# Routing order, unread products and the weight tiles of the first layer in a two-layer mixer and expert kernel

## The chip, the cores and the metric

The kernel runs on 1 core of one Trainium2 chip. The metric is device time in microseconds (us), the median of the runs of one kernel; lower is better. All tensors are float32.

## The reference, cut to what matters

Two layers work on 512 latent rows and 256 context rows of 1024 columns. Each layer first mixes tokens (four head groups, output projection, gated residual) and then runs expert-choice experts, which the change touches:

```python
def expert_choice_ffn(x, router_w, wg, wu, wd):
    bn, n, _ = x.shape
    cap = CAPACITY_FACTOR * n // N_EXPERTS
    aff = jax.nn.softmax(jnp.einsum('bnd,de->bne', x, router_w).astype(jnp.float32), axis=-1)
    gate, idx = lax.top_k(aff.transpose(0, 2, 1), cap)
    bidx = jnp.arange(bn)[:, None, None]
    xg = x[bidx, idx]
    hid = jax.nn.silu(jnp.einsum('becd,edf->becf', xg, wg)) * jnp.einsum('becd,edf->becf', xg, wu)
    o = jnp.einsum('becf,efd->becd', hid, wd) * gate[..., None].astype(x.dtype)
    return jnp.zeros_like(x).at[bidx, idx].add(o)
```

There are 16 experts, and each takes the 64 best of the 512 latent rows and, in the first layer, the 32 best of the 256 context rows. The input of the experts is the RMS-normalised row, scaled and shifted by the conditioning. Each expert has three 1024 x 1024 matrices (gate, up, down), 4 MB each; the two layers read 96 of them. The context stream ends after the first layer, so layer 1 (the second) has latent rows alone.

## The kernel before, in words

**Mixers.** Each layer's front computes the projections, the four head groups and the output projection. Its last part, the loop over units `(t, n)`, takes one 128-row tile and 256 columns at a time: `wout_unit` makes the output projection (L1327) and adds it to the residual `X`, and `front_unit`, two units behind, squares the row for the norm (ACT L1345), transposes two 128 x 128 pieces (PE L1348) and multiplies them with the router's weights (PE L1355).

**Routing.** `willing(r)` (r = 0 latent, r = 1 context) turns the sums into the inverse norm (`rsqrt`: ACT L397 and L398, DVE L400 to L403), adds up the logits, and makes the softmax (ACT L1372 is its exponential, DVE L1380 its last step). `route` transposes the affinities (PE L1398), finds the best rows with rounds of max, match-replace and max-index on DVE (L1406 to L1409), and merges two half lists over PE (L1412, L1413, L1417) into row numbers (DVE L1427 to L1437). In layer 0, `fetch` then gathers the chosen rows from DRAM with an indirect DMA (POOL L1452), and `turned` scales a gathered row by its inverse norm (ACT L1464), transposes it (PE L1469), and applies scale and shift: the first four pieces of 128 columns on DVE (L1479), the other four on ACT (L1477). In layer 1 the rows are picked by a matrix product instead (PE L1494, L1472).

The context rows are routed first and gathered while the latent ones are still at work: `xg1 = fetch(1, 0)` stands in the loop, `willing(0)` and `route(True)` behind it, and the context rows are turned into `XC[0]` behind the mark `R0`, the transposes of the latent affinities.

**Experts.** In layer 0 each weight tile is multiplied with 64 latent rows (`lat_mm`, L1587) and 32 context rows (`ctx_mm`, L1595). The first expert's context products come before its latent ones. The hidden state is transposed again before the down matrix (`tr_lat` L1662, `tr_ctx` L1670 to L1671). Every matrix comes in four tiles (`CUTS`), each 1 MB: two rows of 1024 floats on each of 128 partitions. Partition p of a tile holds the neighbouring rows 2p and 2p + 1, so one partition is one piece of 8 KB. To match, whatever is multiplied with a weight tile is cut by `tile_of(k)`: every second column of 256, a slice with step 2.

**Order.** A framework schedules the recorded instructions of each engine by priority and by estimated readiness; each engine then runs its own list strictly in order. `tc.issue_after(x)` puts what is recorded inside it behind instruction x. The weight stream is issued from SP in a fixed order as the arena frees memory; in layer 0 it is held back behind the first gather of latent rows (`st.guard`, a POOL memset at L1562).

Of the kernel before, what the change touches and what calls it, by code (L numbers as in the profile page):

```python
# [226 lines left out]
def hybrid_kernel(ctx: ExitStack, tc: tile.TileContext, T, out):  # L227
# [11 lines left out]
    PS = psp.tile([128, 8, 512], F32, name="banks")  # L239
# [120 lines left out]
    def exp_item(l, e, w, k0, nk, n=None):  # L360

        src = T["exp_w_" + w][l, e]
        if n is None:
            src = src[k0 * 128:(k0 + nk) * 128].rearrange("(p k) f -> p k f", k=2)
            return ("exp", l, e, w, k0), (nk, 1024), lambda ap: sp.dma_start(ap, src)
        src = src[:, n * 512:(n + 1) * 512].rearrange("(q p j) f -> p q j f", p=128, j=2)
        if nk > 1:
            return ("exp", l, e, w, k0, n), (nk, 512), lambda ap: [
                sp.dma_start(ap[:, k:k + 2], src[:, (k0 + k) // 2]) for k in range(0, nk, 2)]
        return ("exp", l, e, w, k0, n), (nk, 512), lambda ap: sp.dma_start(ap[:, 0], src[:, k0 // 2, k0 % 2])  # L370
# [45 lines left out]

    def tile_of(k):

        return slice(k // 2 * 256 + k % 2, k // 2 * 256 + 256, 2)

# [30 lines left out]
    def ada_group(l, b, hf):  # L451
# [14 lines left out]
        for j in range(J):  # L466
            pe.transpose(tb[:, j * 128:(j + 1) * 128], M.v[:, tile_of(j) if b else slice(j * 128, (j + 1) * 128)],
                         ident)
# [63 lines left out]
    def layer(l):  # L532
# [807 lines left out]
        def front_unit(t, n):  # L1340

            r = 0 if t < 4 else 1
            t_ = t - 4 * r
            xs = X.v[:, t, n * 256:(n + 1) * 256]
            act.activation(sqr().v, xs, AF.Square, accum_out=SS[r][:, t_, n:n + 1])  # L1345
            tb = bank("T")
            for kk in range(2):
                pe.transpose(tb[:, kk * 128:(kk + 1) * 128], xs[:, tile_of(kk)], ident)  # L1348
            xt = xq().v
            if t % 2:  # L1350
                dve.tensor_copy(xt, tb[:, 0:256])
            else:
                act.activation(xt, tb[:, 0:256], AF.Copy)
            for kk in range(2):
                pe.matmul(LG[r][:, t_, n], xt[:, kk * 128:(kk + 1) * 128], rwa.v[:, r, 2 * n + kk, :],  # L1355
                          start=kk == 0, stop=kk == 1)

        def willing(r):
# [31 lines left out]
        def route(lat):  # L1390
# [6 lines left out]
            for j in range(nj):  # L1397
                pe.transpose(R[0:64, j * 128:(j + 1) * 128], afl[r].v[:, j].rearrange("p a b -> p (a b)"), ident)  # L1398
            marks["R%d" % r] = nc.cur_bb.bb.instructions[-1]
            wk, tops, tt = rbuf[r]  # L1400
            vals, ix, ixf = tops.v[0:64, 0], tops.v[0:64, 1].bitcast(U32), tops.v[0:64, 2]
# [53 lines left out]

        def turned(r, xg, d=None, halves=(0, 1)):

            d = d or (xtr if r == 0 else xtc)()
            fetched = isinstance(xg, Buf)
            for k4 in halves:  # L1460
# [4 lines left out]
                for kk in range(4):  # L1465
                    k = k4 * 4 + kk
                    o = tb[:, kk * 128:(kk + 1) * 128]
                    if fetched:
                        pe.transpose(o, xg.v[:, tile_of(k)], ident)  # L1469
                    else:  # L1470
                        for t in range(4):
                            pe.matmul(o, X.v[:, t, tile_of(k)], xg[:, t], start=t == 0, stop=t == 3)  # L1472
                for kk in range(4):
                    k = k4 * 4 + kk
                    a, b = modA[l][:, 1, k, r:r + 1], modT[l][:, 3, k, r:r + 1]
                    if k4:
                        act.activation(d.v[:, k, :], tb[:, kk * 128:(kk + 1) * 128], AF.Identity, scale=a, bias=b)  # L1477
# [69 lines left out]
        st.limit = AHEAD[1][l] + MORE[l]  # L1547
        st.pump()
        willing(0)
        rt[0] = route(True)  # L1550
        mp = latest(mybir.EngineType.PE)
        kinds["T"][0] = [5, 6]
        if cx:
            xg0 = fetch(0, 0)
            gi = latest(mybir.EngineType.Pool)
            with tc.issue_after(marks["R0"]):
                XC[0] = turned(1, xg1).v
            XG[0] = turned(0, xg0).v
# [100 lines left out]
        def tr_lat(h1):  # L1659
            tb = bank("T")  # L1660
            for j in range(4):
                pe.transpose(tb[:, j * 128:(j + 1) * 128], h1[:, tile_of(j)], ident)  # L1662
            a = ht()
# [4 lines left out]
        def tr_ctx(h2):  # L1668
            tb = bank("T")
            for i in range(4):  # L1670
                pe.transpose(tb[:, i * 64:(i + 1) * 64], h2[:, tile_of(i)], ident[0:64, 0:64])  # L1671
            c = htc()
# [303 lines left out]
def _arrays(v):  # L1976
# [11 lines left out]
    pack = lambda *ts: np.concatenate([t.reshape(t.shape[0], -1) for t in ts], 1)  # L1988
    a["c0"] = pack(np.eye(128, dtype=np.float32), cc, np.stack([rows(v["norm1_g"]), twos(v["norm2_g"])], 2))
    dg = np.stack([v["diff_qn_g"], v["diff_kn_g"]], 1)  # L1990
# [3 lines left out]
    for l in range(DEPTH):  # L1994
        rw = np.zeros((128, 8, 16), np.float32)
        rw[:] = v["router_w"][l].reshape(4, 128, 2, NE).transpose(1, 0, 2, 3).reshape(128, 8, NE)
        sgb = v["sgu_b"][l].reshape(2, 2, 128).transpose(1, 0, 2)
# [24 lines left out]
```

## Time and profile before

| | |
|---|---|
| median of 3 runs | 1990.66 us (1985.25, 1990.66, 2001.73) |
| profiled execution, its own time | 1998.31 us |
| its span, first to last instruction | 1996.2 us |
| mean granted TensorE clock | 0.963 |
| PE / DVE / ACT / POOL busy | 1818.0 / 898.0 / 651.6 / 226.7 us |
| experts of layer 0, products of latent rows | 546.9 to 1107 us |
| experts of layer 1, products | 1533.6 to about 1984 us |

The profile's busy times are averages over stages with different limits: the two fronts (to about 546 us, and from 1107 to 1533 us) are chains over several engines, the experts of layer 0 keep TensorE busy throughout, and those of layer 1 run at the pace of the weight stream. TensorE's granted clock has two levels, 1.0 (2.4 GHz) and 0.5 (1.2 GHz).

### The profile page before, as it was taken

To read this page: it belongs to the slowest core of one execution; us is meant where nothing else is said; L and a number is where in the kernel's file an instruction comes from. 1 tells how busy PE (TensorE), PEld (TensorE's weight loads), DVE (VectorE), ACT (ScalarE), POOL (GpSimd) and SP (SyncE) were. 2 spreads that over 40 slices of the span, in tenths; PEclk is the share of its full clock that TensorE was granted. 3 is DMA by queue.
4 is the path that set the end of the run, shared out by engine and by line. 5 is a ranking of instruction groups with operands and counts; after the bars stand their busy time and mean duration, and the time that the engine had idled before them with its cause. 6 is when DMAs were issued, how large, how long until landed. Compare 5 with 4: busy or idle time off the path is not lost.

```text
span 1996.2 us, 31498 instructions
## 1 busy us (share of the span) xinstructions
PE 1818.0 (91%) x13005; PEld 1028.0 (52%) x13005; DVE 898.0 (45%) x1885; ACT 651.6 (33%) x1386; POOL 226.7 (11%) x191
## 2 busy tenths in 40 slices
PE   5999988989699999999999799898896999988888
PEld 3786787679433333333333388596694333322322
DVE  3758564533523433433434565864434243223222
ACT  2456544532222322322222345654520221111101
POOL 0432033101000000000000043232010000000000
PEclk9999999979799999999999899998887999999999
DMA  9116135542599999988988212525727999999997
GB/s 337 55 50 199 43 114 173 194 147 85 197 413 393 384 336 358 377 331 340 365 335 331 82 43 94 168 93 195 274 102 252 421 421 421 421 422 422 422 422 306
DMA packets 131967, 525.98 MB, mean 263 GB/s; under 512 B 12240, under 2 KB 42864, under 8 KB 83184
## 3 DMA queue, kind: packets, MB, share of 16 engines
q1 hardware_dynamic: 129088, 514.00, 67.0%
q0 software_dynamic: 2736, 9.97, 1.3%
q8 instruction: 102, 1.67, 0.3%
q14 instruction: 41, 0.34, 0.0%
HBM read 513.40 MB, written 10.52 MB: 262 GB/s over the span
## 4 chain that ended last, share of the span: by engine, by line
PE 31%; DMA 16%; DVE 4%; ACT 2%; issue 1%; SPq 1%; POOL 0%; ACTq 0%; DVEq 0%; POOLq 0%
PE banks L1587 13%; DMA ar<-in_exp_w_gate 5%; DMA ar<-in_exp_w_up 5%; DMA ar<-in_exp_w_down 4%; PE banks L1595 3%; PE banks L1327 3%; PE banks L628 1%; DMA ar<-in_w_in 1%; PE banks L697 1%; PE banks L639 1%; PE banks L1718 1%; PE banks L1036 1%; PE banks L458 1%; PE banks L1719 1%; SPq L1030 1%
## 5 line engine op out<-in xcount | busy, mean ns | idle before, releaser
L1587 PE MATMUL banks<-ar,ar 128*32 128x512 f32 (+1 forms) x4576 | 713.6, 597 | 31.6 <-DMA ar<-in_exp_w_down 14.1
L1587 PEld LDWEIGHTS banks<-ar,ar 128*32 128x32 f32 (+1 forms) x4576 | 195.1, 119 | 454.6 <-issue 379.8
L1595 PE MATMUL banks<-ar,ar 128*32 128x512 f32 x1536 | 203.7, 605 | 0.0
L628 PE MATMUL banks<-ar,ar 128*128 128x256 f32 x1344 | 175.8, 287 | 2.0 <-DVE ar L807 1.5
L628 PEld LDWEIGHTS banks<-ar,ar 128*128 128x128 f32 x1344 | 166.7, 193 | 7.1 <-issue 2.6
L1327 PE MATMUL banks<-ar,ar 128*128 128x256 f32 x960 | 140.4, 302 | 1.9 <-ACT ar L1223 1.3
L1327 PEld LDWEIGHTS banks<-ar,ar 128*128 128x128 f32 x960 | 128.4, 204 | 4.0 <-ACT ar L1223 2.4
L1721 DVE TENSOR_TENSOR ar<-ar,banks 128x512 f32<-128x512 f32 x136 | 87.5, 683 | 67.5 <-PE banks L1719 67.2
L1595 PEld LDWEIGHTS banks<-ar,ar 128*32 128x32 f32 x1536 | 51.0, 112 | 117.3 <-issue 108.8
L1452 POOL DMA_INDIRECT ar<-rows,icoli x19 | 18.0, 949 | 783.0 <-ACT ar L1477 457.1
L408 ACT ACTIVATE ar<-banks 128x512 f32<-128x512 f32 x32 | 19.1, 597 | 255.4 <-PE banks L1587 255.4
L1685 DVE SCALAR_TENSOR_TENSOR ar<-banks,gcol,ar 64x512 f32<-64x512 f32 x62 | 46.5, 749 | 124.3 <-PE banks L1587 123.6
L571 POOL TENSOR_TENSOR ar<-ar,ar 128x2048 fp32r<-128x2048 f32 x14 | 64.7, 4625 | 180.1 <-ACT ar L570 166.4
L1477 ACT ACTIVATE ar<-banks,modT,modA 128x128 f32<-128x128 f32 x80 | 30.1, 456 | 167.6 <-PE banks L1469 136.3
L458 PE MATMUL banks<-ar,S 128*32 128x256 f32 x768 | 62.7, 403 | 21.2 <-DMA ar<-in_ada_w 20.2
L697 PE MATMUL banks<-ar,ar 128*128 128x512 f32 (+1 forms) x288 | 72.0, 397 | 4.8 <-DVE ar L598 2.0
L906 ACT ACTIVATE ar<-banks,mx 128x768 f32<-128x768 f32 (+1 forms) x80 | 65.2, 819 | 31.4 <-DVE mx L903 29.0
L411 DVE SCALAR_TENSOR_TENSOR ar<-banks,ar 128x512 f32<-128x512 f32 x32 | 21.9, 683 | 117.1 <-ACT ar L410 117.1
L903 DVE TENSOR_REDUCE mx<-banks 128x1 f32<-128x768 f32 (+1 forms) x80 | 66.6, 845 | 15.0 <-PE banks L898 12.1
L1656 DVE TENSOR_TENSOR ar<-banks,ar 64x512 f32<-64x512 f32 x32 | 21.7, 679 | 97.3 <-ACT ar L1601 97.3
L639 PE MATMUL banks<-ar,ar 128*128 128x512 f32 (+1 forms) x288 | 62.6, 372 | 2.4 <-ACT ar L815 2.3
L697 PEld LDWEIGHTS banks<-ar,ar 128*128 128x128 f32 x288 | 51.8, 197 | 17.5 <-DVE ar L582 2.8
(341 smaller groups left out, 2505.5 us busy)
## 6 DMA issues: line engine op xcount, KB each, us to landing
ar<-in_exp_w_gate SPq DMA_DIRECT2D x128, 1024.0 KB
ar<-in_exp_w_up SPq DMA_DIRECT2D x128, 1024.0 KB
ar<-in_exp_w_down SPq DMA_DIRECT2D x124, 1024.0 KB
ar<-in_ada_w SPq DMA_DIRECT2D x96, 512.0 KB
ar<-in_w_in SPq DMA_DIRECT2D x18, 1024.0 KB
ar<-in_w_out SPq DMA_DIRECT2D x8, 1024.0 KB
ar<-in_exp_w_down SPq DMA_DIRECT2D x7, 512.0 KB
ar<-in_rpb SPq DMA_DIRECT2D x8, 384.0 KB
```

The costliest lines, as they stand in the source:

```text
L458: pe.matmul(B[32 * q:32 * q + 32, 0:n], S[:, k, :], w[:, q * n:(q + 1) * n], start=k == 0, stop=k == 7)
L571: pool.tensor_tensor(lo, raw, hi.v, OP.subtract)
L628: pe.matmul(B[:, tt * 256:(tt + 1) * 256], a.r[:, k, t * 128:(t + 1) * 128], b[:, k, :], start=n == 0, stop=n == 23)
L639: pe.matmul(B[:, 0:n1 - n0], b[:, k, c * 128:(c + 1) * 128], a.r[:, k, n0:n1], start=n == 0, stop=n == 23)
L697: pe.matmul(PS[:, t, s], x.r[:, k, t * 128:(t + 1) * 128], w, start=k == 0 and i == 0, stop=k == 7 and i == 2)
L903: dve.tensor_reduce(mx, s, AX, OP.max, negate=True)
L906: act.activation(e, s, AF.Exp, bias=mx, accum_out=sm)
L1327: pe.matmul(B, a[:, c, t * 128:(t + 1) * 128], b[:, k, :], start=i == 0, stop=i == 23)
L1587: pe.matmul(B[n * 64 + j:n * 64 + j + p, :], xt[:, k, j:j + p], w[:, k - k0, n * 512:(n + 1) * 512], start=k == 0, stop=k == 7)
L1595: pe.matmul(B[j:j + 32, :], xt[:, k, :], w[:, k - k0, n * 512:(n + 1) * 512], start=k < 2, stop=k > 5)
L1685: dve.scalar_tensor_tensor(o[p0:p0 + 64, n * 512:(n + 1) * 512], B[s, :], gc[s, e:e + 1], G2.v[s, 0, n * 512:(n + 1) * 512], OP.mult, OP.mult)
L1721: dve.tensor_tensor(xs, xs, B, OP.add)
```

## The change

1. **Order in the routing of layer 0.** The exponential of the latent softmax is marked (`E0`), and the turning of the context rows is placed behind that mark too, no longer behind `R0` alone. The scale and shift of `XC[0]` all go to ACT (`spare=True`).
2. **Unread products.** `warm(n)` multiplies a piece of X with the identity n times, into a bank that nobody reads: twice ahead of `willing(0)` in both layers, and behind the transposes of the latent affinities four times in layer 0 and eight times in layer 1.
3. **Weight tiles of layer 0.** A tile's two rows per partition are p and p + 128, so that each 128-row tile is a block of neighbouring rows, and one partition is two pieces of 4 KB. `tile_of(k, l)` gives in layer 0 plain slices of 128 neighbouring columns; the norm gains, the router's weights and the conditioning are laid out to match. Layer 1 keeps its layout.

```diff
     def exp_item(l, e, w, k0, nk, n=None):
 
         src = T["exp_w_" + w][l, e]
+        if l + 1 < DEPTH:
+            src = src[k0 * 128:(k0 + nk) * 128].rearrange("(k p) f -> p k f", p=128)
+            return ("exp", l, e, w, k0), (nk, 1024), lambda ap: sp.dma_start(ap, src)
         if n is None:
             src = src[k0 * 128:(k0 + nk) * 128].rearrange("(p k) f -> p k f", k=2)
...
-    def tile_of(k):
-
+    def tile_of(k, l):
+
+        if l + 1 < DEPTH:
+            return slice(k * 128, (k + 1) * 128)
         return slice(k // 2 * 256 + k % 2, k // 2 * 256 + 256, 2)
...
+        def warm(n):
+
+            with tc.issue_after(latest(mybir.EngineType.PE)):
+                for _ in range(n):
+                    pe.matmul(PS[:, 1, :], ident, X.v[:, 0, 0:512], start=True, stop=True)
 
         def willing(r):
...
             act.activation(lgb, lgb, AF.Exp)
+            marks["E%d" % r] = latest(mybir.EngineType.Activation)
...
             marks["R%d" % r] = nc.cur_bb.bb.instructions[-1]
+            if lat:
+                warm(4 if cx else 8)
...
-        def turned(r, xg, d=None, halves=(0, 1)):
+        def turned(r, xg, d=None, halves=(0, 1), spare=False):
...
-                        pe.transpose(o, xg.v[:, tile_of(k)], ident)
+                        pe.transpose(o, xg.v[:, tile_of(k, l)], ident)
...
-                    if k4:
+                    if k4 or spare:
                         act.activation(d.v[:, k, :], tb[:, kk * 128:(kk + 1) * 128], AF.Identity, scale=a, bias=b)
...
         st.pump()
+        warm(2)
         willing(0)
         rt[0] = route(True)
...
-            with tc.issue_after(marks["R0"]):
-                XC[0] = turned(1, xg1).v
+            with tc.issue_after(marks["R0"]), tc.issue_after(marks["E0"]):
+                XC[0] = turned(1, xg1, spare=True).v
             XG[0] = turned(0, xg0).v
```

The same `tile_of(k, l)` stands in `front_unit`, `tr_lat`, `tr_ctx` and the conditioning's transposes (L467).

The lists of the engines show what the scheduler made of it. ScalarE (ACT) at the routing of layer 0, before; `n20y` is the inverse norm of the latent rows, `lg_4942` their logits, `ar_4042` the gathered context rows, `ar_4921` is `XC[0]`, `ar_4043` the first gathered latent rows, L1601 copies half of a context product:

```order
L397 ACTIVATE n20y<-n20v 128x4
L1464 ACTIVATE ar_4042<-ar_4042 128x512 x2
L398 ACTIVATE n20y<-n20y 128x4
L1372 ACTIVATE lg_4942<-lg_4942 128x64
L1477 ACTIVATE ar_4921<-banks,modT_73,modA_75 128x128 x4
L1601 ACTIVATE ar_4912<-banks 64x512
L408 ACTIVATE ar_4909<-ar_4912 64x512
L409 ACTIVATE ar_4909<-ar_4909 64x512
L410 ACTIVATE ar_4909<-ar_4909 64x512
L412 ACTIVATE ar_4909<-ar_4909 64x512
L1464 ACTIVATE ar_4043<-ar_4043 128x512 x2
L1601 ACTIVATE ar_4913<-banks 64x512
```

and with the change (line numbers are those of the changed kernel, L1478 is L1464 of before):

```order
L400 ACTIVATE n20y<-n20v 128x4
L401 ACTIVATE n20y<-n20y 128x4
L1383 ACTIVATE lg_4944<-lg_4944 128x64
L1478 ACTIVATE ar_4042<-ar_4042 128x512 x2
L1491 ACTIVATE ar_4921<-banks,modT_73,modA_75 128x128 x8
L1616 ACTIVATE ar_4912<-banks 64x512
L411 ACTIVATE ar_4909<-ar_4912 64x512
L412 ACTIVATE ar_4909<-ar_4909 64x512
L413 ACTIVATE ar_4909<-ar_4909 64x512
L415 ACTIVATE ar_4909<-ar_4909 64x512
L1616 ACTIVATE ar_4913<-banks 64x512
L1478 ACTIVATE ar_4043<-ar_4043 128x512 x2
```

The scaling of the gathered context rows stands behind the softmax's exponential, all eight pieces of `XC[0]` are ACT's, and the copy of the second context product (L1601, now L1616) has come ahead of the scaling of the first latent rows.

VectorE (DVE) at the end of the latent list of best rows in layer 0, before; L1656 and L411 belong to the first expert's context rows, `cand` and `icol` to the merged list:

```order
L1406 MAX ar_4005<-ar_4004 64x8
L411 SCALAR_TENSOR_TENSOR ar_4909<-ar_4912,ar_4909 64x512
L1409 MAX_INDEX ar_4005<-ar_4005,ar_4004 64x8
L1410 CAST ar_4005<-ar_4005 64x64
L1650 TENSOR_TENSOR ar_4909<-ar_4909,ar_4912 64x512
L1414 COPY ar_4006<-banks 64x128
```

and with the change:

```order
L1423 MAX_INDEX ar_4005<-ar_4005,ar_4004 64x8
L1671 TENSOR_TENSOR ar_4912<-banks,ar_4912 64x512
L1424 CAST ar_4005<-ar_4005 64x64
L1428 COPY ar_4006<-banks 64x128
L1441 COPY cand_4998<-banks 128x64
L1443 TENSOR_TENSOR late_4996<-cand_4998 128x16
L1444 SCALAR_TENSOR_TENSOR dif_4997<-cand_4998 128x16
L1452 TENSOR_TENSOR gcol_4995<-cand_4998 128x16
L1445 TENSOR_TENSOR dif_4997<-dif_4997,late_4996 128x16
L414 SCALAR_TENSOR_TENSOR ar_4909<-ar_4912,ar_4909 64x512
L1448 TENSOR_TENSOR icol_4994<-dif_4997,cand_4998 64x8 x2
```

L1656 (now L1671) moved from among the rounds to behind the last one, L411 (now L414) from ahead of the last round to just ahead of the row numbers, and L1650 behind them.

TensorE (PE) in the same place with the change; L1367 are the unread products, L1610 (L1595 before) the first context products:

```order
L1360 MATMUL banks<-ar_3989,ar_3997 128x16 x2
L1367 MATMUL banks<-ar_3918,c_68 128x512 x2
L1410 MATMUL banks<-c_68,ar_4002 64x128 x2
L1367 MATMUL banks<-ar_3918,c_68 128x512 x4
L1483 MATMUL banks<-c_68,ar_4042 128x128 x8
L1610 MATMUL banks<-ar_4054,ar_4921 32x512 x4
```

Apart from the two L1367 rows this list is as before: the four products stand ahead of the context rows' transposes.

## Rows read from the trace of the kernel before

**Rows 1.** The page, part 1: busy time (share of the span) and instructions.

```profile
PE 1818.0 (91%) x13005; PEld 1028.0 (52%) x13005; DVE 898.0 (45%) x1885; ACT 651.6 (33%) x1386; POOL 226.7 (11%) x191
```

**Rows 2.** Windows, experts of both layers: length, engines, PEclk, DMA share, GB/s.

```profile
546.88:1107.20 560.32, 557.07 (x4789) 189.18 (x4788) 222.09 (x357) 149.64 (x268) 8.43 (x9) 1.00 0.92 356
1550.00:1900.00 350.00, 319.92 (x1412) 112.51 (x1412) 104.40 (x171) 59.63 (x107) 6.61 (x7) 1.00 1.01 422
```

**Rows 3.** Timeline, softmax of layer 0: start, duration, instruction [idle before <-releaser].

```profile
514.40 0.20 ACT L397 ACTIVATE n20y<-n20v 128x4 f32<-128x4 f32 x1 [0.44 <-DVE n20v L395]
518.86 1.33 ACT L1464 ACTIVATE ar<-ar 128x512 f32<-128x512 f32 x2 [4.26 <-DMA ar<-rows,icoli]
520.10 0.19 ACT L398 ACTIVATE n20y<-n20y 128x4 f32<-128x4 f32 x1
...
523.37 0.63 PE L1398 MATMUL banks<-c,ar 128*64 128x128 f32 x2 [7.78 <-DVE ar L1380]
```

**Rows 4.** Timeline, layer 0, from the list of best rows to the first latent rows.

```profile
524.90 0.73 DVE L1479 TENSOR_SCALAR ar<-banks,modA,modT 128x128 f32<-128x128 f32 x2
...
525.75 1.50 ACT L1477 ACTIVATE ar<-banks,modT,modA 128x128 f32<-128x128 f32 x4 [3.16 <-PE banks L1469]
...
529.91 0.59 ACT L1601 ACTIVATE ar<-banks 64x512 f32<-64x512 f32 x1 [2.66 <-PE banks L1595]
...
531.94 0.66 DVE L1656 TENSOR_TENSOR ar<-banks,ar 64x512 f32<-64x512 f32 x1
...
535.35 0.67 DVE L411 SCALAR_TENSOR_TENSOR ar<-ar,ar 64x512 f32<-64x512 f32 x1
...
538.63 6.00 PE L1595 MATMUL banks<-ar,ar 128*32 128x512 f32 x32
...
539.88 0.17 DVE L1437 CAST icoli<-icol 128x8 int32<-128x8 f32 x1
...
545.59 1.36 PE L1469 MATMUL banks<-c,ar 128*128 128x128 f32 x8 [0.95 <-ACT ar L1464]
```

**Rows 5.** Timeline, the same steps in layer 1.

```profile
1503.90 0.20 ACT L397 ACTIVATE n20y<-n20v 128x4 f32<-128x4 f32 x1 [0.44 <-DVE n20v L395]
...
1507.91 0.63 PE L1398 MATMUL banks<-c,ar 128*64 128x128 f32 x2 [2.82 <-DVE ar L1380]
1518.20 0.31 PE L1412 MATMUL banks<-c,ar 64*64 64x64 f32 x1 [9.65 <-DVE ar L1406]
...
1521.86 0.17 DVE L1437 CAST icoli<-icol 128x8 int32<-128x8 f32 x1
...
1524.38 9.32 PE L1472 MATMUL banks<-ar,ar 128*128 128x128 f32 x56 [0.79 <-DVE ar L1496]
```

**Rows 6.** Windows of the two routings: columns as in Rows 2.

```profile
516.00:518.00 2.00, 0.00 (x0) 0.00 (x0) 0.06 (x1) 0.00 (x0) 0.00 (x0) 0.53 0.98 338
1528.00:1530.00 2.00, 2.00 (x11) 2.00 (x11) 0.00 (x0) 0.00 (x0) 0.00 (x0) 0.53 0.00 0
```

**Rows 7.** Timeline of PE, layer 1: products of this form, identity and X.

```profile
1945.15 1.02 PE L1744 MATMUL banks<-ar,c 128*128 128x512 f32 x2
1946.01 1.02 PE L1741 MATMUL banks<-ar,c 128*128 128x512 f32 x2
```

**Rows 8.** One line, L467: durations in ns (min/median/max) of weight loads.

```profile
L467 PEld LDWEIGHTS banks<-c,ar x24: 137/196/219, 26.4 to 1426.0; 128*128 128x128 f32 x24
```

**Rows 9.** Timeline of PE: transposes of step 2 (L1469, L1662) and of neighbouring columns (L920).

```profile
162.39 0.82 PE L920 MATMUL banks<-c,ar 128*128 128x128 f32 x6
...
173.07 0.60 PE L920 MATMUL banks<-c,ar 128*128 128x128 f32 x4
...
565.90 0.75 PE L1662 MATMUL banks<-c,ar 128*128 128x128 f32 x4
...
662.78 1.23 PE L1469 MATMUL banks<-c,ar 128*128 128x128 f32 x8
```

**Rows 10.** Lines, 546.88 to 1107.2 us, PE: count, busy us, mean ns.

```profile
L1469 PE MATMUL banks<-c,ar 128*128 128x128 f32 x81 | 12.6, 296 | 0.0
L1662 PE MATMUL banks<-c,ar 128*128 128x128 f32 x64 | 11.9, 308 | 0.0
```

**Rows 11.** Windows with short DMA pieces: columns as in Rows 2.

```profile
25.00:50.00 25.00, 21.58 (x140) 13.48 (x140) 10.44 (x26) 5.54 (x16) 2.51 (x2) 0.93 0.90 327
1960.00:1970.00 10.00, 9.21 (x40) 2.97 (x39) 1.38 (x2) 0.00 (x0) 0.00 (x0) 1.00 1.01 410
```

**Rows 12.** Waits, 545 to 1110 us: in total, times, longest.

```profile
PEld banks L1587 <- DMA ar<-in_exp_w_down: 1.3, 4, 0.4
```

More of the change, by code (lines that the diff above doesn't have):

```diff
@@ L466, in ada_group @@
         for j in range(J):
-            pe.transpose(tb[:, j * 128:(j + 1) * 128], M.v[:, tile_of(j) if b else slice(j * 128, (j + 1) * 128)],
+            pe.transpose(tb[:, j * 128:(j + 1) * 128], M.v[:, tile_of(j, l) if b else slice(j * 128, (j + 1) * 128)],
                          ident)
@@ L1347, in front_unit @@
             for kk in range(2):
-                pe.transpose(tb[:, kk * 128:(kk + 1) * 128], xs[:, tile_of(kk)], ident)
+                pe.transpose(tb[:, kk * 128:(kk + 1) * 128], xs[:, tile_of(kk, l)], ident)
             xt = xq().v
@@ L1468, in turned @@
                     if fetched:
-                        pe.transpose(o, xg.v[:, tile_of(k)], ident)
+                        pe.transpose(o, xg.v[:, tile_of(k, l)], ident)
                     else:
                         for t in range(4):
-                            pe.matmul(o, X.v[:, t, tile_of(k)], xg[:, t], start=t == 0, stop=t == 3)
+                            pe.matmul(o, X.v[:, t, tile_of(k, l)], xg[:, t], start=t == 0, stop=t == 3)
                 for kk in range(4):
@@ L1661, in tr_lat @@
             for j in range(4):
-                pe.transpose(tb[:, j * 128:(j + 1) * 128], h1[:, tile_of(j)], ident)
+                pe.transpose(tb[:, j * 128:(j + 1) * 128], h1[:, tile_of(j, l)], ident)
             a = ht()
@@ L1670, in tr_ctx @@
             for i in range(4):
-                pe.transpose(tb[:, i * 64:(i + 1) * 64], h2[:, tile_of(i)], ident[0:64, 0:64])
+                pe.transpose(tb[:, i * 64:(i + 1) * 64], h2[:, tile_of(i, l)], ident[0:64, 0:64])
             c = htc()
@@ L1988, in _arrays @@
     pack = lambda *ts: np.concatenate([t.reshape(t.shape[0], -1) for t in ts], 1)
-    a["c0"] = pack(np.eye(128, dtype=np.float32), cc, np.stack([rows(v["norm1_g"]), twos(v["norm2_g"])], 2))
+    a["c0"] = pack(np.eye(128, dtype=np.float32), cc, np.stack(
+        [rows(v["norm1_g"]), np.concatenate([rows(v["norm2_g"][:-1]), twos(v["norm2_g"][-1:])], 1)], 2))
     dg = np.stack([v["diff_qn_g"], v["diff_kn_g"]], 1)
@@ L1995, in _arrays @@
         rw = np.zeros((128, 8, 16), np.float32)
-        rw[:] = v["router_w"][l].reshape(4, 128, 2, NE).transpose(1, 0, 2, 3).reshape(128, 8, NE)
+        by = (4, 128, 2, NE) if l + 1 == DEPTH else (4, 2, 128, NE)
+        rw[:] = np.moveaxis(v["router_w"][l].reshape(by), by.index(128), 0).reshape(128, 8, NE)
         sgb = v["sgu_b"][l].reshape(2, 2, 128).transpose(1, 0, 2)
```

## The prediction, made before the changed kernel ran

> **What bounds the kernel now.** I read the page first: TensorE is busy 91% of the span [rows 1], but an average over four stages says nothing about the routing. The windows separate them [rows 2]. In the experts of layer 0 PE is busy 557.07 of 560.32 us while the DMA moves 356 GB/s; in those of layer 1 the DMA's share is 1.01 at 422 GB/s. So time saved on PE counts in the first of these stages and not in the second. The two routings lie ahead of them, and there the timeline shows which wait ends last.
>
> In layer 0 the latent softmax is held up by work that isn't its own: ACT does L397 at 514.40, then stands in front of L1464, which waits 4.26 us for the gathered context rows, and comes to L398 at 520.10. The affinities reach PE (L1398) at 523.37, 8.97 us after L397 [rows 3]. Layer 1 has the same steps and no gathered rows: there it is 1507.91 - 1503.90 = 4.01 us [rows 5]. The rounds that find the best rows then share DVE with foreign work: four pieces of L1479, L1656 and L411 stand among them [rows 4].
>
> PE rests in both routings and its clock falls: 0.53 in the mean at 516 to 518, where it has no product, and still 0.53 at 1528 to 1530, where it is busy again [rows 6].
>
> **The change, part by part.**
>
> *Softmax ahead of the scaling.* From L397 to L1398 I take layer 1's 4.01 in place of 8.97: -4.96 us, L1398 at 518.4. From L1398 to the row numbers (L1437) layer 0 takes 539.88 - 523.37 = 16.51 us and layer 1, on an undisturbed DVE, 1521.86 - 1507.91 = 13.95. By the new order L1656 and L411 still lie on this chain, 0.66 + 0.67: 15.28, so -1.23. Together L1437 comes at 533.7, **6.2 us earlier** [rows 3 to 5].
>
> The new wait is L1656 itself. It stands in the queue of the last step, behind it the cast, the merge and all that follows, and it needs the first context product, which now starts behind four unread products. One call of this form is two instructions, 1946.01 - 1945.15 = 0.86 us [rows 7]. From L1398's end at 519.0 PE needs 3.4 us, then 1.2 for eight transposes [rows 9]; ACT, 0.6 us in, takes 8 x 0.375 = 3.0 (four took 1.50), and L1601 began 2.66 us behind the last of these [rows 4]. So L1656 is ready near 529.3. DVE reaches it 10.3 us after L1398 by layer 1's pace (1518.20 - 1507.91 [rows 5]) and a last index search later, 529.1. There is no margin, so I count -6.0.
>
> Behind L1437 the gather is as before: 545.59 - 539.88 = 5.7 us to the first transposes of latent rows. The second context batch, 6.00 us before [rows 4], and its copy, which now stands ahead of the scaling on ACT, must fit under it: PE starts them once the merge is off it, some 2 us ahead of L1437, so near 531.7; they end by 537.7 and the copy, 0.59, by 538.3; the scaling, 0.7 us ahead of the first transposes as for the context rows, would begin at 533.7 + 5.7 - 0.7 = 538.7. This cover is thin too. The POOL memset that lets the weight stream go on sits behind the same gather, so it moves with it, and SP's queue with that.
>
> *Pieces of XC[0] to ACT.* Four pieces leave DVE (0.73 for two, [rows 4]); that gain is in the 1.23 above. ACT has 1.5 us more, counted above.
>
> *Unread products.* PE's pauses ahead of L1398 begin at 523.37 - 7.78 = 515.6 and at 1505.1 [rows 3, 5]. Two calls, 1.7 us, lie in what remains of them, up to 518.4 and 1507.9. In layer 1 eight calls, 6.9 us from 1508.5, are done at 1515.4, ahead of L1412 at 1518.20 [rows 5, 7]. All of it is in pauses: cost 0. If PE ran them at the low level, eight would take 13.8 us, end at 1522.3 and hold L1412 up by 4.1 us. What they can give is bounded by L1472: 9.32 us for 56, of which the part to about 1530 is at the low level [rows 5, 6]; at the high one at most half of these 5.6 us goes, -2.8. Between their end and the dense products at 1522 PE has a few small ones only, and after a pause like that the clock had fallen [rows 6]. I take 0 here, and 0 for a higher clock in layer 0's routing.
>
> *Neighbouring columns in the transposes.* The data are the loaded weights of these products. On one line and one form, L467, with plain slices in a third of its calls and step 2 in the others, loading takes 137 to 219 ns [rows 8]. In the stream, four transposes of step 2 take 0.75 (L1662) and four of neighbouring columns 0.60 (L920), so 64/4 = 16 groups save 0.15 each, 2.4 us. Eight of step 2 take 1.23; six of the other kind 0.82, or 0.11 for each further one, so eight are 1.04: ten groups of L1469 save 0.19 each, 1.9 us [rows 9, 10]. All lie in the stage where PE is the bound: **-4.3 us**. Bounds: 0, if load time hides behind the products around it, and -6.7, if the 16 groups of `tr_ctx` save 0.15 too.
>
> The Trainium skill, page "TensorE: Matmul & The Clock Gate", section "LDWEIGHTS (loading the stationary operand)", speaks against this term: it gives the load time by the number of columns alone, so a step would cost nothing. The spread within L467 disagrees with it; by the page this term would be 0.
>
> *Weight tiles in pieces of 4 KB.* The same bytes in twice as many pieces. The nearest row is the last matrix, in 2 KB pieces among others: 410 GB/s, against 422 for 8 KB [rows 11, 2]. Layer 0 needs 356 (359 once it is 4.3 us shorter), so any value between the two is hidden behind PE, which waited 1.3 us in all for the down matrices [rows 12]. Cost 0. If that cover goes, each per cent of rate below 359 costs 5.6 us.
>
> *Sum.* -6.0 - 4.3 = **-10.3 us**. It passes on: layer 0's products end earlier, layer 1's front is the same chain from there, and its stream restarts when its first products free their tiles. The profiled execution's own time is 1998.31 (its span 1996.2 and 2.1 around it), which makes 1988.0. It is 7.65 above the median of the runs, 1990.66, so the median should be **1980** (1990.66 - 10.3 = 1980.4).
>
> **The rivals.**
>
> - *The step costs nothing on the path.* The loads overlap the products before them, and PE's time per group stays. For it: PEld is busy only 189 of 560 us [rows 2]. Against it: the groups themselves are longer [rows 9]. Then -6.0 alone, 1984.7. This is also what the page above would make of it.
> - *The unread products are in the way.* They run at the low level, at 1.72 a call. In layer 0 four take 6.9 us, L1656 is ready some 3.5 to 4 us later, and about 2 of the 6.0 remain; in layer 1, 4.1 us are lost. -2 + 4.1 - 4.3 = -2.2: 1988.5. For it: the clock fell in just these pauses [rows 6]. Against it: two calls now stand in the pause ahead.
> - *More than I count.* The clock holds into L1472 (-2.8) and `tr_ctx` saves as well (-2.4): -15.5, 1975.
> - *Slower: the weight stream becomes the bound of layer 0.* The stretch moves 356 x 560.3 = 199.5 MB. If 4 KB pieces go at the 327 GB/s seen at 25 to 50 us among short pieces [rows 11], that takes 610 us, 50 more, less the 6 that it starts earlier: +44, 2035. It begins to count at 359 GB/s, and is slower than before by 20 us at 340. Against it: the share there was 0.90, so 327 is not what the pieces allow, and 2 KB pieces made 410.
>
> **How the numbers follow.** Forecast 0.54, step free 0.15, products in the way 0.14, more 0.12, slower 0.05. A measurement of this kernel can tell about 1%, 20 us, from no change. Forecast and first two rivals lie within it; faster by over 1% needs most of "more" or a favourable draw of runs that themselves spread over 16 us: 0.12. Slower by over 1% is the stream's case: 0.05. Same: 0.83. The range goes from the fourth case less 6 us of spread, 1969, to just above the third, 1991; it leaves out the stream's case and tails of the others.
>
> **What would show it.** Right: ACT's L1372 near 517.4, ahead of L1464, which still starts near 518.9; L1437 near 533.7 and the first latent transposes near 539.9; no wait of DVE at L1656; groups of L1662 at 0.60 and of L1469 at 1.04; PE still without pause to about 1097, with DMA around 360 GB/s there. Wrong: DVE idle ahead of L1656, L1412 behind the last unread product, group times unchanged, or waits of the layer 0 products for weights.

## The result, and the profile after

The changed kernel takes **1980.94 us** in the median of 20 runs (1973.37 to 1984.69), the kernel before 1991.99 in 20 runs beside it (1983.15 to 2006.09). The ratio is **0.9938**, 95% interval [0.9924, 0.9952]: 12.3 us less, between 9.6 and 15.1. The forecast was 1980 and -10.3. The profiled execution of the changed kernel took 1984.42 us (span 1982.3), 3.5 above its median. Its lines are numbered anew: L1464, L1469 and L1477 became L1478, L1483 and L1491, L1398 became L1410, L1437 is L1451, L1587 and L1595 are L1602 and L1610, L1656 is L1671, L1662 is L1677, and the former L1671 (the transposes in `tr_ctx`) is L1686. The unread products are L1367.

The page's part 1 of the changed kernel: busy time, share, instructions.

```profile
PE 1825.0 (92%) x13037; PEld 1022.3 (52%) x13037; DVE 897.6 (45%) x1881; ACT 653.7 (33%) x1390; POOL 228.4 (12%) x191
```

Beside [rows 1] this says almost nothing: PE is even busier, by the unread products. The windows say where the time went. First the experts of layer 0 of the changed kernel, first product of latent rows to last, and the stretch of layer 1 as in [rows 2]:

```profile
539.78:1104.84 565.06, 561.39 (x4885) 184.73 (x4888) 221.72 (x356) 149.98 (x269) 8.43 (x9) 1.00 0.94 353
...
1550.00:1900.00 350.00, 317.43 (x1398) 110.79 (x1396) 103.90 (x170) 56.63 (x102) 5.62 (x6) 1.00 1.01 422
```

and the kernel before, also from its first product of latent rows in layer 0 to its last:

```profile
546.88:1120.35 573.47, 569.03 (x4885) 193.10 (x4888) 223.21 (x359) 150.02 (x269) 8.43 (x9) 0.99 0.90 348
```

The stage is 8.4 us shorter for the same 4885 instructions of PE. That the weight loads are busy 8.4 us less too (193.10 to 184.73) is a coincidence: they overlap the products, and what they save shows on the path in part only, as is worked out at the end. Layer 1 still runs at the stream's 422 GB/s.

The routing of layer 0 in the changed kernel, as a timeline (to be laid beside [rows 3, 4]):

```profile
512.59 0.20 ACT L400 ACTIVATE n20y<-n20v 128x4 f32<-128x4 f32 x1 [0.44 <-DVE n20v L398]
...
515.58 0.26 ACT L1383 ACTIVATE lg<-lg 128x64 f32<-128x64 f32 x1 [2.54 <-DVE lg L1382]
515.74 1.32 ACT L1478 ACTIVATE ar<-ar 128x512 f32<-128x512 f32 x2
...
517.08 0.38 PE L1410 MATMUL banks<-c,ar 128*64 128x128 f32 x2
517.30 3.60 PE L1367 MATMUL banks<-ar,c 128*128 128x512 f32 x8
...
520.74 1.04 PE L1483 MATMUL banks<-c,ar 128*128 128x128 f32 x8
...
521.37 2.90 ACT L1491 ACTIVATE ar<-banks,modT,modA 128x128 f32<-128x128 f32 x8 [4.32 <-PE banks L1483]
...
525.91 0.59 ACT L1616 ACTIVATE ar<-banks 64x512 f32<-64x512 f32 x1 [1.63 <-PE banks L1610]
...
527.51 0.67 DVE L1671 TENSOR_TENSOR ar<-banks,ar 64x512 f32<-64x512 f32 x1
...
531.23 0.17 DVE L1451 CAST icoli<-icol 128x8 int32<-128x8 f32 x1
...
532.26 1.34 POOL L1466 DMA_INDIRECT ar<-rows,icoli  x1 [22.09 <-DVE ar L1500]
...
537.88 1.97 PE L1483 MATMUL banks<-c,ar 128*128 128x128 f32 x8 [3.04 <-ACT ar L1478]
```

The scaling L1478 now stands behind the exponential L1383 and waits for nothing. From L400 (the former L397) to L1410 it is 4.49 us in place of 8.97; from there to the row numbers 531.23 - 517.08 = 14.15 in place of 16.51; from the row numbers to the first latent transposes 6.65 in place of 5.71. In all, first expert product included: 27.19 us in place of 32.48.

The transposes in the stream of the changed kernel, timeline and then lines (545 to 1100 us):

```profile
581.02 1.09 PE L1483 MATMUL banks<-c,ar 128*128 128x128 f32 x8
...
592.48 0.66 PE L1677 MATMUL banks<-c,ar 128*128 128x128 f32 x4
593.07 0.46 PE L1686 MATMUL banks<-c,ar 64*128 64x64 f32 x4
...
L1677 PE MATMUL banks<-c,ar 128*128 128x128 f32 x64 | 10.5, 286 | 0.0
L1686 PE MATMUL banks<-c,ar 64*128 64x64 f32 x64 | 7.3, 234 | 3.7 <-DVE ar L1834 3.7
```

The group of `tr_ctx` in the kernel before, which [rows 9] did not have:

```profile
566.58 0.69 PE L1671 MATMUL banks<-c,ar 64*128 64x64 f32 x4
```

A group of eight fell from 1.23 to 1.09, one of four from 0.75 to 0.66, and that of `tr_ctx` most of all, from 0.69 to 0.46.

### The profile page after: what moved, and what is told of

The parts are those of the page before. It is cut to its first block, busy times and chain, and to the rows that moved or that the text cites. A ratio compares the mean times of both kernels' runs of the same rounds, so it can differ in the third digit from the quotient of the medians.

```text
span 1982.3 us, 31560 instructions
## 1 busy us (share of the span) xinstructions
PE 1825.0 (92%) x13037; PEld 1022.3 (52%) x13037; DVE 897.6 (45%) x1881; ACT 653.7 (33%) x1390; POOL 228.4 (12%) x191
## 4 chain that ended last, share of the span: by engine, by line
PE 33%; DMA 15%; DVE 4%; ACT 2%; issue 1%; SPq 1%; POOL 0%; ACTq 0%; DVEq 0%; POOLq 0%
PE banks L1602 15%; DMA ar<-in_exp_w_gate 4%; DMA ar<-in_exp_w_down 4%; DMA ar<-in_exp_w_up 4%; PE banks L1610 3%; PE banks L1332 2%; DMA ar<-in_w_in 2%; PE banks L633 1%; PE banks L702 1%; PE banks L644 1%; PE banks L1733 1%; PE banks L463 1%; PE banks L1734 1%; SPq L1035 1%; PE banks L1486 0%
## 5 line engine op out<-in xcount | busy, mean ns | idle before, releaser
L1602 PE MATMUL banks<-ar,ar 128*32 128x512 f32 (+1 forms) x4576 | 714.1, 598 | 32.9 <-DMA ar<-in_exp_w_down 14.0
L1602 PEld LDWEIGHTS banks<-ar,ar 128*32 128x32 f32 (+1 forms) x4576 | 194.6, 119 | 457.2 <-issue 379.0
L1610 PE MATMUL banks<-ar,ar 128*32 128x512 f32 x1536 | 201.2, 598 | 0.1
L633 PEld LDWEIGHTS banks<-ar,ar 128*128 128x128 f32 x1344 | 166.7, 193 | 7.2 <-issue 2.6
L1332 PEld LDWEIGHTS banks<-ar,ar 128*128 128x128 f32 x960 | 125.8, 201 | 4.4 <-ACT ar L1228 2.4
L1610 PEld LDWEIGHTS banks<-ar,ar 128*32 128x32 f32 x1536 | 50.8, 111 | 115.8 <-issue 107.9
L411 ACT ACTIVATE ar<-banks 128x512 f32<-128x512 f32 x32 | 19.1, 597 | 256.3 <-PE banks L1602 256.3
L1491 ACT ACTIVATE ar<-banks,modT,modA 128x128 f32<-128x128 f32 x84 | 31.5, 458 | 169.4 <-PE banks L1483 138.4
L414 DVE SCALAR_TENSOR_TENSOR ar<-banks,ar 128x512 f32<-128x512 f32 x32 | 21.9, 683 | 112.0 <-ACT ar L413 112.0
L1671 DVE TENSOR_TENSOR ar<-banks,ar 64x512 f32<-64x512 f32 x32 | 21.8, 680 | 95.1 <-ACT ar L1616 95.1
L1679 DVE COPY ar<-banks 128x512 f32<-128x512 f32 x32 | 22.1, 691 | 91.0 <-PE banks L1677 91.0
```

The lines of the kernel that those rows point to most:

```text
L633: pe.matmul(B[:, tt * 256:(tt + 1) * 256], a.r[:, k, t * 128:(t + 1) * 128], b[:, k, :], start=n == 0, stop=n == 23)
L1332: pe.matmul(B, a[:, c, t * 128:(t + 1) * 128], b[:, k, :], start=i == 0, stop=i == 23)
L1602: pe.matmul(B[n * 64 + j:n * 64 + j + p, :], xt[:, k, j:j + p], w[:, k - k0, n * 512:(n + 1) * 512], start=k == 0, stop=k == 7)
L1610: pe.matmul(B[j:j + 32, :], xt[:, k, :], w[:, k - k0, n * 512:(n + 1) * 512], start=k < 2, stop=k > 5)
```

## The experiments

All have their kernel before beside them. Stage lengths are read from one profile of each: A is from L397 to the first product of latent rows in layer 0, B from there to the end of the last one, C from there to L397 of layer 1. In e6, e7 and e9 weight rows meet other columns than theirs, so that part of what they compute differs; the products are as many.

| kernel | order | unread | columns | pieces | ratio | A | B | C |
|---|---|---|---|---|---|---|---|---|
| before | old | - | step 2 | 8 KB | 1 | 32.48 | 573.47 | 383.55 |
| e5 before again | old | - | step 2 | 8 KB | one run | 29.24 | 571.90 | 381.07 |
| e1 | new | - | step 2 | 8 KB | 0.9987 [0.9969, 1.0005] | 27.48 | 573.00 | 380.09 |
| e4 | new | yes | step 2 | 8 KB | 0.9997 [0.9975, 1.0018] | 27.36 | 572.52 | 383.75 |
| e7 | old | - | step 2 | 4 KB | 1.0003 [0.9986, 1.0021] | 29.04 | 570.39 | 380.94 |
| e9 | old | - | neighbours | 8 KB | 0.9960 [0.9945, 0.9975] | 28.85 | 565.45 | 380.76 |
| e2 | old | - | neighbours | 4 KB | 0.9929 [0.9902, 0.9957] | 28.90 | 564.81 | 381.10 |
| e6 | new | yes | neighbours | 8 KB | 0.9973 [0.9958, 0.9988] | 26.99 | 570.15 | 384.46 |
| e3 | new | - | neighbours | 4 KB | 0.9922 [0.9897, 0.9947] | 27.07 | 565.62 | 380.10 |
| e11, e3 again | new | - | neighbours | 4 KB | 0.9950 [0.9933, 0.9967] | 25.98 | 564.97 | 383.64 |
| changed | new | yes | neighbours | 4 KB | 0.9938 [0.9924, 0.9952] | 27.19 | 565.06 | 383.87 |
| e10 late unread | new | layer 1 | neighbours | 4 KB | 0.9955 [0.9938, 0.9971] | 26.27 | 565.17 | 384.66 |
| e8 layer 1 too | new | yes | neighbours | 4 KB | 1.0013 [0.9999, 1.0027] | 26.69 | 566.55 | 379.56 |

**e1, the order alone.** To the kernel before:

```diff
+            marks["E%d" % r] = latest(mybir.EngineType.Activation)
...
-                    if k4:
+                    if k4 or spare:
...
-            with tc.issue_after(marks["R0"]):
-                XC[0] = turned(1, xg1).v
+            with tc.issue_after(marks["R0"]), tc.issue_after(marks["E0"]):
+                XC[0] = turned(1, xg1, spare=True).v
```

> The new order of the latent softmax and the pieces of XC[0] on ACT, without unread products and with the old weight tiles. Theory (two separate gains, at the routing of layer 0 and in the transposes of layer 0's experts): the stretch from L397 to the first latent product, 32.5 us before, shortens by 5 to 6.5; time against before -5 to -7 us. Rival (the unread products are needed: without them the clock falls and the first context products come late for L1656): the list of best rows waits for L1656, and only -2 to -3 us remain.

Measured 0.9987: 2.6 us less where 5 to 7 were expected, and no change lies inside the interval, although A is 5.0 us shorter than in the profile of the kernel before.

**e2, the tiles alone** (its lines are those of e7 and e9 below, with the layouts of the router's weights and of the norm's gains that go with them).

> The tiles of 128 neighbouring rows in layer 0 alone: old order, no unread products. Theory: the groups of transposes shorten by 0.09 (L1662), 0.13 (L1469) and 0.24 us (tr_ctx), 16, 10 and 16 of them, so layer 0's stage of latent products is 6 to 7 us shorter, and time against before is -6 to -7 us. Rival (the rest of the 8.4 us of that stage, and perhaps more, is a clock that fell there in one profile and not in the other): -3 us or less.

Measured 0.9929, 14 us less where 6 to 7 were expected: the tiles carry the gain. But A is 3.6 us shorter here too, with the old order.

**e3, without the unread products**, and **e4, without the tiles** (the lines of e2 taken back). e3 to the changed kernel:

```diff
-            if lat:
-                warm(4 if cx else 8)
...
-        warm(2)
```

> The changed kernel without its unread products. Theory: they lie in pauses and give under 1 us: time against before -11 to -13 us, as with them. Rival (they keep the clock up for the first context products and for L1398 to L1417): against the changed kernel 2 to 4 us are lost, -8 to -10 against before, seen as a wait of DVE ahead of L1656 or a longer stretch from L1398 to L1437 in layer 0.

> The changed kernel with the old weight tiles: order and unread products alone. Theory: -5 to -7 us against before, and groups of L1662 at 0.75 us again. Rival (the transposes are not the second gain): -9 us or more.

Measured 0.9922 and 0.9997. The unread products give nothing that can be measured; without the tiles nothing of the gain is left, where 5 to 7 us were expected from the order.

**e5, the kernel before once more**, unedited.

> The kernel before once more, for one look. Six profiles so far show the gathered context rows of layer 0 landing 2.3, 2.3, 3.4, 4.0, 4.2 and 5.6 us after their first packet, among weight pieces that start 1.3 to 1.9 us behind them; the one of 5.6 us is the profile of the kernel before, on which the routing term rests. Theory A (the landing is a matter of chance, and the profile of before had the longest): here it lands in another time, most likely 2.3 to 4.2 us, the scaling on ACT waits 0.9 to 2.9 us in place of 4.26, and latent softmax sum to its division on ACT (L397 to L1372 of before) takes 4.6 to 6.5 us in place of 7.94; so what the new order is worth varies between executions and is about 3 us in the mean, not 5. Theory B (the kernel before always waits like that): landing 5.6 us, wait 4.2 us, 7.9 us again.

1990.57 us. ACT's timeline in this second execution, to be laid beside [rows 3]:

```profile
513.98 0.21 ACT L397 ACTIVATE n20y<-n20v 128x4 f32<-128x4 f32 x1 [0.44 <-DVE n20v L395]
515.28 1.33 ACT L1464 ACTIVATE ar<-ar 128x512 f32<-128x512 f32 x2 [1.09 <-DMA ar<-rows,icoli]
516.52 0.19 ACT L398 ACTIVATE n20y<-n20y 128x4 f32<-128x4 f32 x1
518.75 0.26 ACT L1372 ACTIVATE lg<-lg 128x64 f32<-128x64 f32 x1 [2.04 <-DVE lg L1371]
```

Theory A holds. L1464 waits 1.09 us, not 4.26, and L397 to L1372 is 4.77, not 7.94. The four other profiles with the old order have 28.85 to 29.24 in A; the 32.48 on which the routing term stood belonged to one execution. The new order has 25.98 to 27.48, mean 26.88. It is worth 29.0 - 26.9 = 2.1 us in A against these four, and 2.8 against all five (mean 29.7).

**e6 and e7, the two halves of the tiles.** e6 is the changed kernel with 8 KB pieces, e7 the kernel before with 4 KB pieces. The lines that e6 leaves out are the ones that e7 adds:

```diff
+        if l + 1 < DEPTH:
+            src = src[k0 * 128:(k0 + nk) * 128].rearrange("(k p) f -> p k f", p=128)
+            return ("exp", l, e, w, k0), (nk, 1024), lambda ap: sp.dma_start(ap, src)
```

> The changed kernel with the weight tiles of the first layer loaded in 8 KB pieces as before (row 2p + k in partition p), while the products still take neighbouring columns: in the experts of layer 0 weight rows meet other columns than theirs, so that part of what is computed differs. Theory A (the gain of the tiles is the stepped columns alone, and 4 KB pieces are hidden): ratio to before 0.9938 +- 0.003 as the changed kernel; products of layer 0, first to last, 565 us; four transposes of the context's hidden rows 0.59 us. Rival B (the smaller pieces bring the gain, or part of it): products 573 us and a ratio of about 0.999. Rival C (the 4 KB pieces cost something): up to 0.5% below the changed kernel.

> The kernel before with only the weight tiles of layer 0 in 4 KB pieces (rows k*128 + p), the columns still taken with step 2: weight rows meet other columns than theirs in the experts of layer 0, so that part of what is computed differs. Theory A (4 KB pieces are hidden): ratio 1.000 +- 0.003, products of layer 0 573 us. Rival B (the smaller pieces bring the gain): 0.993, 565 us. Rival C (they let the gathered rows of the context through sooner, since a packet ahead of them on a queue is half as long): landing near 2.3 us in place of 5.6, the scaling's wait 0.9 us, products unchanged: -2 to -3.5 us.

e7: 1.0003, nothing; the first gather lands in 2.6 us, as its rival C says, but so it does in e5 with 8 KB pieces (2.5). e6: 0.9973 and 570.15 in B, between its theory A and its rival B. Its trace says where the stage lost time. Timeline of e6, the gathered rows for expert 11 (POOL, ACT) and the transposes of `tr_ctx` behind them:

```profile
942.45 0.94 POOL L1463 DMA_INDIRECT ar<-rows,icoli  x1 [70.59 <-issue]
...
952.74 1.33 ACT L1475 ACTIVATE ar<-ar 128x512 f32<-128x512 f32 x2 [5.76 <-DMA ar<-rows,icoli]
...
956.18 0.46 PE L1683 MATMUL banks<-c,ar 64*128 64x64 f32 x4 [2.29 <-DVE ar L1831]
```

ACT stands 5.76 us in front of rows that were asked for 10.3 us earlier, its next work comes late, and PE waits 2.29 us in a stage in which it is the bound. In the first profile of before the scaling began 6.2 us after the gather and this wait is missing; in e5 it was 9.9 us and PE stood 1.79 us longer than usual there. In e6 three groups of `tr_ctx` wait 6.5 us in all, in e2 one waits 2.8, that of the last expert, which waits 2.7 to 2.9 in every profile. This leaves open whether 8 KB pieces make the other waits likelier, so the fourth combination of columns and pieces was run.

**e9, neighbouring columns alone, with 8 KB pieces**, on the kernel before:

```diff
-    def tile_of(k):
+    def tile_of(k, l):
+        if l + 1 < DEPTH:
+            return slice(k * 128, (k + 1) * 128)
```

> The kernel before with only the neighbouring columns in the transposes of layer 0; the weight tiles stay in 8 KB pieces, so that in its experts weight rows meet other columns than theirs and part of what is computed differs. With the steps of the kernel before, the step-2 columns with 4 KB pieces and both together this is the last corner of a square of four. Theory A (the columns are the whole gain, the pieces cost and give nothing, and what else differed came with the gathered rows and the clock by chance): each expert 0.3 to 0.6 us shorter, products of layer 0 from 572 to 566 us, ratio 0.9955 to 0.997, more where the front is lucky too. Rival B (only both together give the gain): products 570 us, ratio 0.998 to 1.000.

0.9960 and B at 565.45: theory A. The window of its B, and its two lines (545 to 1100 us):

```profile
542.70:1108.15 565.45, 560.91 (x4885) 185.02 (x4888) 223.10 (x359) 150.09 (x269) 8.44 (x9) 1.00 0.92 353
...
L1664 PE MATMUL banks<-c,ar 128*128 128x128 f32 x64 | 10.5, 286 | 0.0
L1673 PE MATMUL banks<-c,ar 64*128 64x64 f32 x64 | 7.3, 234 | 4.5 <-DVE ar L1821 4.5
```

Busy time and means are those of the changed kernel. From one `tr_ctx` group to the next, undisturbed experts take the same time whatever the pieces: 33.62, 37.36 and 34.92 us with step 2 (before, e7), 33.17, 37.05 and 34.33 with neighbouring columns (e6, e9, e2, changed). So the columns are the gain of the undisturbed experts, and there the pieces have no price.

In the disturbed ones shorter pieces help. What an execution adds to the shortest of these intervals (from the first group of `tr_ctx` to that of the 15th expert) is 1.8 to 3.7 us in the six profiles with 8 KB pieces and 0.0 to 1.8 in the seven with 4 KB, 2.4 and 0.9 in the mean. The gather near 800 us shows where it comes from. POOL and ACT in the kernel before, then in the changed one:

```profile
806.67 0.94 POOL L1452 DMA_INDIRECT ar<-rows,icoli  x1 [70.05 <-PE banks L1469]
...
815.38 1.34 ACT L1464 ACTIVATE ar<-ar 128x512 f32<-128x512 f32 x2 [2.22 <-DMA ar<-rows,icoli]
```

```profile
797.16 0.94 POOL L1466 DMA_INDIRECT ar<-rows,icoli  x1 [69.27 <-PE banks L1483]
...
804.36 1.33 ACT L1478 ACTIVATE ar<-ar 128x512 f32<-128x512 f32 x2 [0.83 <-DMA ar<-rows,icoli]
```

From the gather to the scaling of its rows it is 8.7 us here with 8 KB pieces and 7.2 with 4 KB; the six profiles have 8.2 to 8.7, the seven 7.2 to 7.8. The times agree in sign: with neighbouring columns the two kernels with 8 KB pieces are at 0.9960 and 0.9973, the five with 4 KB at 0.9922 to 0.9955, in the mean 0.3% or some 5 us lower. The traces show 1.6 us of this. The rest stays open, and with step 2 e7 shows none of it, within 0.0018 of its ratio (3.5 us).

**e8, layer 1 in such tiles too** (the condition `l + 1 < DEPTH` goes from the load, from `tile_of`, and from the layouts of the router's weights and the norm's gains).

> The changed kernel with the experts' weights of layer 1 too in tiles of 128 neighbouring rows (4 KB pieces, neighbouring columns). Theory A (in layer 1 the stream is the bound, so shorter transposes give nothing there and the price of the pieces shows): a 4 KB packet takes 159 ns where one of 8 KB takes 309, 2.9% more for the same bytes, on some 410 us of stream: +12 us against the changed kernel, ratio to before about 1.000, layer 1 from its first product to the end 475 us in place of 463. Rival B (the transposes count there too, and the pieces cost nothing): as in layer 0, -6 us more: 0.991, 457 us. Rival C (both without effect): 0.994, 463 us.

1.0013, by the ratios 15 us more than the changed kernel (0.0075 of 1990). From the first product of layer 1 to the end it is 474.34 us in place of 464.15. The window of layer 1 in e8, against the 422 GB/s above:

```profile
1550.00:1900.00 350.00, 309.59 (x1362) 103.71 (x1361) 102.49 (x168) 55.29 (x100) 5.62 (x6) 1.00 1.03 410
```

Theory A: where the stream is the bound, the 4 KB pieces cost some 3% of the rate, and nothing of shorter transposes is seen. In layer 0 the same pieces hide behind PE.

**e10, unread products later and longer in layer 1, none in layer 0**, and **e11, e3 again**, on the same chip. e10 to the changed kernel:

```diff
-        warm(2)
+        if not cx:
+            warm(2)
...
-            if lat:
-                warm(4 if cx else 8)
+            if lat and not cx:
+                warm(11)
...
+            if lat and not cx:
+                warm(4)
             va, ia, vb, ib = (R3[...
```

> The changed kernel with the unread products of layer 0 left out and those of layer 1 spread over the whole of its routing: two calls ahead of the affinities' transposes as now, 11 behind them in place of 8 (22 instructions at 0.44 us: 9.7 us, done just ahead of the next transpose 10.0 us on), and 4 behind the merge (3.5 us of the 3.7 before the gathering products). Theory A (the clock stays at the high level through the routing): the 56 gathering products take 6 us or less in place of 8.73, the first expert product of layer 1 comes 2.5 to 3 us earlier after its softmax, and, if the stream starts again from there, the end too: ratio to before 0.9915, 2 us below the version without unread products. Rival B (the stream is the bound): the products come earlier, the end does not; 0.9925. Rival C (they run at the low level and stand in the way): the second transpose of the routing up to 8 us later, 0.996.

> The changed kernel without its unread products, a second time, beside the version with late ones and on the same chip. Theory A (the unread products as written give nothing): ratio to before 0.992 as the first time, at or below the 0.9938 of the changed kernel. Rival B (the first time was luck): 0.994 or above.

PE's timeline in layer 1 of e10:

```profile
1499.50 9.61 PE L1367 MATMUL banks<-ar,c 128*128 128x512 f32 x22
...
1511.24 3.70 PE L1367 MATMUL banks<-ar,c 128*128 128x512 f32 x8
...
1516.16 6.86 PE L1488 MATMUL banks<-ar,ar 128*128 128x128 f32 x56 [0.78 <-DVE ar L1512]
```

The granted clock of the 56 gathering products is 1.00 here against 0.76 in the changed kernel, and they take 6.86 us in place of 8.73. The stage from L397 to the first product of layer 1 is 28.20 us, in place of 29.41 in the changed kernel and 29.27 in e11. In the time nothing of it is seen: 0.9955, beside 0.9950 for e11. So the mechanism of theory A is there, but is worth a microsecond. And e11 came out as its rival B: the 0.9922 of e3, the same kernel, was in part a favourable draw. No version beats the changed kernel beyond the intervals.

## Why the prediction was right

The number was right, and the two terms behind it were both mis-sized, in opposite directions: that -10.3 came so near is in part luck.

- **Softmax ahead of the scaling, -6.0 forecast.** Against the profiled execution it is -5.3 (A: 32.48 to 27.19), and up to the row numbers the path is the one described: L1383 ahead of L1478, and no wait at L1671, whose inputs were there before DVE came to it. Against what the kernel before usually does it is -2.1. Two steps failed. The first is "From L397 to L1398 I take layer 1's 4.01 in place of 8.97": the 8.97 held a wait of 4.26 us for gathered rows, and their landing took 5.6 us after their first packet in that execution, 2.1 to 4.2 in the twelve others. The second is "Behind L1437 the gather is as before". Besides the row numbers the gather waits for the inverse norms, which it reads with the rows and which SP writes to DRAM (L1383, now L1395). Timelines of the kernel before, of the changed kernel, and of e6, where the view names the write as what ended the wait:

```profile
521.11 0.38 SPq L1383 DMA_DIRECT2D rows<-n20y  x1
```

```profile
517.21 2.25 SPq L1395 DMA_DIRECT2D rows<-n20y  x1
```

```profile
532.17 0.94 POOL L1463 DMA_INDIRECT ar<-rows,icoli  x1 [23.07 <-DMA rows<-n20y]
```

By the semaphore events of the traces this write had landed 3.0 to 6.1 us ahead of the row numbers in the five profiles with the old order, and the gather began 0.27 us behind the end of L1437. In all eight with the new order the write is the last to come: the gather begins 0.74 us behind its landing, and 0.5 to 2.4 us (mean 1.2) behind the row numbers. In the changed kernel the write lands 14.3 us after its issue, at 531.52, when the row numbers have been ready for 0.1 us; the L1500 that POOL's line in the timeline of the result names is not what the gather waited for. So part of what the new order gains up to the row numbers is lost again in front of the gather. Two smaller pieces: L1410 to L1451 took 14.15, not 15.28; and the first latent transposes then ran at the low level (granted clock 0.50, 1.97 us for eight).
- **Part of that comes back in the front of layer 1.** With the old order C is 380.8 to 381.1 in four of five profiles; with the new order it is 379.6 to 380.1 in three and 383.6 to 384.7 in five. The step "layer 1's front is the same chain from there" of the sum does not hold. From some 250 us behind the last product of layer 0 on, the engines' lists differ there, though no line of the edit to the order stands in that front: the five profiles with the old order share one list and the eight with the new order another (on PE apart from the unread products). On DVE 45 of the 547 places up to the first product of layer 1 hold another instruction. The windows of a place 262 us behind the last product of layer 0 show one cause of the two lengths; first e5 with the old list, then e3 and the changed kernel with the new one:

```profile
1377.18:1390.88 13.70, 11.61 (x88) 9.06 (x92) 3.91 (x13) 5.23 (x13) 0.00 (x0) 0.75 1.03 396
```

```profile
1365.97:1379.67 13.70, 12.64 (x80) 9.77 (x81) 3.45 (x12) 5.48 (x14) 0.00 (x0) 0.76 0.97 369
```

```profile
1366.90:1380.60 13.70, 11.66 (x51) 8.97 (x52) 2.02 (x8) 4.07 (x11) 0.00 (x0) 0.50 1.03 400
```

With the new list PE gets 51 instructions through at a granted clock of 0.50, and 80 at 0.76. Which of the two an execution meets changed between e3 and e11, the same kernel. The low one (0.50 to 0.53) stands in five of the eight profiles with the new list and in none of the five with the old (0.75 each); that is no proof that the new list brings it about. So 2.1 us in A, less some 1 us in C, is what e1 shows as 2.6 +- 3.6.
- **Neighbouring columns, -4.3 forecast.** B fell from 572.3 (mean of the five profiles with step 2) to 565.4 (of seven with neighbouring columns): -6.9. The eighth, e6 with its waits, is left out of this; with it the mean is 566.0. By line, from one start to the next, in the kernels before and changed: L1469 11.56 to 10.22 (-1.3, forecast -1.9), the former L1671 9.87 to 6.19 (-3.7, forecast 0, with 2.4 in the bound), L1662 16 x 0.09 (-1.4, forecast -2.4). The choice that failed is to leave `tr_ctx` out of the sum because no row of neighbouring columns had its shape: it was the largest piece. And 0.60 for four such transposes, read at L920, was too low for the stream, where they take 0.66. The router's transposes save another 1.0 us in the front of layer 0, which the prediction didn't count: from the first L1355 to the end of the last it is 72.5 us in place of 73.5.
- **The rival "the step costs nothing"** fell: in e9 the loads for `tr_ctx` are at 137 ns in place of 208, and the groups are shorter. The section "LDWEIGHTS (loading the stationary operand)" of the Trainium skill's page "TensorE: Matmul & The Clock Gate" gives the load time by the number of columns alone; these loads have 128 columns either way, and the traces disagree with it.
- **4 KB pieces, 0**: right for the undisturbed experts of layer 0 (e7, e9). Left out was what they do for gathered rows among them, 1.6 us in the mean. The slower rival's mechanism is real, and e8 is the place where it decides.
- **Unread products, 0**: right. Behind the affinities' transposes of layer 0 they run at the high level, 0.45 us an instruction, and are over before PE is wanted; "in the way" did not come about there. The two calls ahead run at a granted clock of 0.54 (3.62 us for four instructions) and hold L1410 back by 0.5 us in the changed kernel (4.49 us from L397, against 3.97 in e3), which the wait for the write of the inverse norms hides. Nor did the gain of the fourth rival: from the first gathering product of layer 1 to the first expert product it is 8.66 us with them and 8.82 in e3 without.

In the time the terms add up to -2.1 + 1 - 6.9, and some -0.8 ahead of L397 (mean of eight profiles against five, spread 7), or about -9, where -12.3 [-15.1, -9.6] was measured. The missing 3 us are not placed; one profile of each kernel is too little for that.

## What to carry to other kernels

A wait for a gather among a weight stream is a draw, not a property: before a term is built on one, look at the same wait in a second execution or at its sisters in the program, and price it by their middle. Before work ahead of a gather is shortened, go through everything else that the gather waits for: here a small write with 3 us to spare became the bound. A stepped slice as the stationary operand of an fp32 transpose is worth a look wherever PE is the bound, first of all where few columns move. And the same edit has opposite signs in two layers of one program, when PE bounds the one and the stream the other.

## What the runs showed that was not expected

- A step of 2 in the stationary fp32 operand makes its load longer by half, with 64 rows and with 128. The loads for `tr_ctx` before and in the changed kernel, by lines (545 to 1100 us; mean ns behind the busy time):

```profile
L1671 PEld LDWEIGHTS banks<-c,ar 64*128 64x128 f32 x60 | 8.3, 208 | 3.5 <-DVE ar L1819 1.8
```

```profile
L1686 PEld LDWEIGHTS banks<-c,ar 64*128 64x128 f32 x64 | 5.1, 137 | 6.5 <-DVE ar L1834 4.1 <-issue 2.3
```

The two other lines went from 207 and 209 to 140 ns. What of these 70 ns a load is seen on the path depends on the product beside it: with 64 moving columns (`tr_ctx`) 3.7 us of 64 x 71 ns = 4.5, with 128 (L1469, L1662) 2.7 of 144 x 68 ns = 9.8.
- Halving the packets from 8 KB to 4 KB cost some 3% of the stream's rate at its bound (422 to 410 GB/s).
- A write of 512 inverse norms of 4 bytes each, issued by SP among the weight stream, landed 12.9 to 18.2 us after its issue (13 profiles).
- Two executions of one kernel differ by 3 us and more in a stage by the granted clock or by the landing of one gather alone. A single profile can't tell such a difference from an edit's.
